# Hybrid decoder layer: low probability parts moved from VectorE to GpSimd, causal mask from a TensorE product to a VectorE addition in PSUM

## The chip, the core and the metric

The kernel is one program on one core of a Trainium2 chip. The core has TensorE (PE: matrix products, with its weight loads shown apart as PEld), VectorE (DVE), ScalarE (ACT), GpSimd (POOL) and SyncE (SP, which here only issues DMAs). Each engine works through its own queue in order; semaphores hold an instruction back until what it needs is there. The metric is the time on the device in microseconds (us), lower is better.

## What is computed

A decoder layer over 2048 tokens of width 1024, in fp32. The input is normalised and modulated, projected once, and feeds two attention branches: eight "forgetting" heads (causal softmax attention with a bias from cumulated log forget gates) and eight sliding-window heads. Each branch is gated, both go through one output projection, a second normalisation and a gated residual. The part that the change touches is the forgetting attention:

```python
def one_block(args):
    qb, cb, n = args                                   # 128 queries, their cumulated gate, block number
    s = jnp.einsum('bhqd,bhkd->bhqk', qb, kh, preferred_element_type=jnp.float32) * scale
    s = s + cb[..., None] - cum[:, :, None, :]
    q_pos = n * Q_BLOCK + jnp.arange(Q_BLOCK)
    causal = key_pos[None, :] <= q_pos[:, None]
    s = jnp.where(causal, s, -jnp.inf)
    p = jax.nn.softmax(s, axis=-1)
    return jnp.einsum('bhqk,bhkd->bhqd', p.astype(vh.dtype), vh)
```

## The kernel before

fp32 operands are split into two fp16 parts, a high part (the value rounded to fp16) and a low part (what the rounding left), and a product of two such operands is made of three fp16 products: high x high, high x low, low x high.

The program runs in stages: the modulation and the weights' splitting, the sliding-window branch, the forgetting branch (roughly 462 to 1000 us) and the rest of the output projection (to 1156 us). The forgetting branch also carries most of the projection work of the later heads, which is cut into small units and strewn between the attention's own instructions, so that PE always has something to do.

**Steps.** A forgetting head's 2048 queries are four chunks of 512 (`ci`). A step is one chunk against two blocks of 128 keys, with scores stored transposed: keys on the partitions, queries along the free dimension. Chunk `ci` has 2 x ci + 2 steps, a head 20, all eight heads 160. The last two steps of each chunk cross the diagonal: the first of them holds blocks with 512 and 384 valid queries (896 columns), the second 256 and 128 (384 columns); all others have 1024 columns. These 64 steps (2 x 4 x 8) are called masked steps here. `self.blocks` lists each block with its first valid sub-block `u0` and its column offset `o`.

**Life of a step** (class `Step`, line 1331 on):
- `scores` (L1339): for each of the two blocks two products into one PSUM tile `sta` (L1349 the low parts against the high ones, L1350 the rest with the gate's bias rows), and for a block on the diagonal a third, L1352: identity x `dmaskT`, a 128 x 128 constant with 0 where the key is allowed and -1e30 where it isn't, added into the block's first 128 columns. There is one `sta` tile (two banks), so the next step's scores wait until this step's exponential has read it.
- `exp32` (L1356, ACT): the exponential from PSUM to an fp32 tile `p`.
- `high` (L1360, ACT): `p` rounded to fp16, the first half of tile `pha`.
- `low` (L1363, DVE): `p` minus the rounded value, in fp16, the second half of `pha`. Both tiles have three buffers.
- `pv` (L1373, L1375, L1376, PE): the products with the values; L1376 reads the low part. After a chunk's last step come L1380 and L1382 (DVE: divide by the row sum) and `o_store` (L283): ACT rounds the output, DVE makes its low part (L291), SP stores it.

**Order of issue.** The program is written out by hand: the loop over `steps` at the end of the function puts each instruction on its engine's queue. One pass `s` issues: the exponential of step s; a `tick`, which issues what was put off by `after` (evacuations of finished units); the low part of step s-1; perhaps a part of the output weights' splitting (`w_out_split`, L1443 on DVE); the first half of this pass's units; the rounding of step s; the scores of step s+1; a second `tick`; the products of step s-2 with the values (`PV_LAG` is 2); the second half of the units. Units are projection units (`proj_units`, three products L351 each, evacuated by ACT and then DVE, L1073 or L392) and row-maximum units (`max_units`: a product L1300, reduced by DVE in L1303 or, for the block on the diagonal, L1305; after a chunk's last one `rows` combines them in L1312 to L1320). They share five PSUM banks.

**GpSimd's queue** holds in this stage only DMA issues: the gate's results (L394), the loads of later weights (L221), their row maxima out to DRAM (`w_max`, L230) and back as a broadcast (`w_back`, L235, which waits for the first to land), and the rows of the output gate (L1231, which wait for DVE to have used the last ones, L1237).

Of the kernel before, what the change touches and what calls it, by code (L numbers as in the profile page):

```python
# [16 lines left out]
ALU = mybir.AluOpType  # L17
AX = mybir.AxisListType

P = 128  # L20
# [15 lines left out]
XM, XR, VW = 66, 69, 129  # L36
# [7 lines left out]
def hybrid_layer(  # L44
# [17 lines left out]
    V, A, G, PE, SP = nc.vector, nc.scalar, nc.gpsimd, nc.tensor, nc.sync  # L62
# [94 lines left out]
    identb = const.tile([P, P], BF16, name="identb")  # L157
    identh = const.tile([P, P], F16, name="identh")
    dmaskT = const.tile([P, P], BF16, name="dmaskT")
# [26 lines left out]
    def bank(hold=False):  # L186
        n = next(n for n in order_ if n not in held)
        order_.remove(n)
        order_.append(n)
        if hold:  # L190
            held.add(n)
        return n
# [270 lines left out]
    start = ExitStack()  # L463
# [409 lines left out]
    class Pair:  # L873
# [7 lines left out]
        def scores(self):  # L881
            self.pss = ps_s.tile([P, 2, CH], F32, tag="s", name="pss")
            q = ab[self.j, self.i // 4]
            for e, (i, k0, nk) in enumerate(self.blocks):
                qo, o = (i % 4) * P, e * 2 * P + (2 - nk) * P
                for n, (a, b) in enumerate(((0, 0), (0, 1), (1, 0))):
                    for h in range(2):
                        r = slice(64 * h, 64 * h + 64)
                        PE.matmul(self.pss[:, h, o:o + nk * P], q[r, a, qo:qo + P],
                                  kst[self.g][r, b, k0 * P:(i + 1) * P], start=(n == 0), stop=(n == 2))  # L890
# [228 lines left out]
    def fill(n, each=None):  # L1119

        for _ in range(n):
            for f in events.pop(pos[0], []):
                f()
            punits[pos[0]]()
            pos[0] += 1
            if each:
                each()
# [120 lines left out]
    def const_rows(n, eng):  # L1248

        for slot, r0, r1 in ((0, 64, 66), (2, 66, 68), (0, 68, 69)):  # L1250
            eng.dma_start(Ts[n][r0:r1, slot, :].rearrange("p (u q) -> p u q", q=P),
                          fx["crow"][r0:r1, :].unsqueeze(1).broadcast_to([r1 - r0, NB, P]))
# [18 lines left out]
    def key_limbs(hd):  # L1271

        cv = sm(NB, "a_cv")
        V.tensor_scalar(cv[:], csum[:, hd, :], isc[f"qk{hd}"][:], None, op0=ALU.mult)
        for col, x_, nx in ((0, XA, True), (1, XB, True), (2, XC, False)):
            lc = lk[:, NB * col:NB * col + NB]
            V.tensor_scalar(lc, cv[:], 1.0 / x_, None, op0=ALU.mult)
            if nx:
                cv2 = sm(NB, "a_cv")
                V.scalar_tensor_tensor(cv2[:], lc, -x_, cv[:], op0=ALU.mult, op1=ALU.add)  # L1280
                cv = cv2
# [49 lines left out]
    class Step:  # L1331
# [9 lines left out]
        def scores(self):  # L1341
            T, ci = Ts[self.hd % 2], self.ci
            self.st = ps_st.tile([P, 2 * CH], F32, tag="st", name="sta")
            for b, u0, o in self.blocks:
                w = CH - u0 * P
                kb_ = slice(b * P, (b + 1) * P)
                qc = slice(ci * CH + u0 * P, (ci + 1) * CH)
                diag = b >= 4 * ci
                PE.matmul(self.st[:, o:o + w], T[:, 3, kb_], T[:, 1, qc], start=True, stop=False)  # L1349
                PE.matmul(self.st[:, o:o + w], T[0:XR, 2, kb_], T[0:XR, 0, qc], start=False, stop=not diag)  # L1350
                if diag:
                    PE.matmul(self.st[:, o:o + P], identb[:], dmaskT[:], start=False, stop=True)  # L1352

        def exp32(self):
            self.p32 = fxp.tile([P, 2 * CH], F32, tag="p32", name="p32")
# [4 lines left out]
            A.activation(self.ph[:, 0, :self.w], self.p32[:, :self.w], AF.Copy)  # L1360

        def low(self):
            V.tensor_tensor(self.ph[:, 1, :self.w], self.p32[:, :self.w], self.ph[:, 0, :self.w], op=ALU.subtract)  # L1363

        def pv(self):
            hd, ph = self.hd, self.ph
# [20 lines left out]
    steps = []  # L1387
# [247 lines left out]
    with tc.manual_schedule():  # L1635
        mi = 0
        V.memset(cmask[:], 0.0)
        V.tensor_copy(cmask[:, 3 * P:], dmask[:])
        const_rows(0, SP)
        const_rows(1, A)  # L1640
        key_limbs(0)
        fill(4, tick)
        pw_ = bk[bank()][:, 0:1]
        PE.matmul(pw_, ones[:], wsum[:], start=True, stop=True)
        root_scale(wrt[:], pw_)
        limbs1, ahead = False, 0
        while pos[0] < N_V3 or mi < M_LEAD:
            fill(1)
            if mi >= M_LEAD - 20 and mi % 2:
                fill(1)  # L1650
                ahead += 1
            if pos[0] == N_QK0 - 22:
                key_rows(0)
            if mi < M_LEAD and pos[0] >= N_QK0 - 12:
                munits[mi]()
                mi += 1
            if pos[0] >= N_V3 - 2 and not limbs1:
                key_limbs(1)
                limbs1 = True
            tick()  # L1660
        for _ in range(3):
            tick()
        key_rows(1)
        steps[0].scores()
        p0 = pos[0] - ahead
        p_tot = N_LAST - p0

        w_at, opened = {}, False
        w_all = sum(s.w for s in steps[:7 * NS])
        w_acc = 0  # L1670
        for s, stp_ in enumerate(steps):
            hd, r = divmod(s, NS)
            w_acc += stp_.w
            npn = p0 + min(p_tot, 14 + p_tot * w_acc // w_all) - pos[0]
            fil = fill
            if hd == 7 and r < 8:
                npn = N_LAST + (len(punits) - N_LAST) * (r + 1) // 8 - pos[0]
            if hd == 7 and r >= 8:
                npn, fil = N_IN * (r - 8) // (NS - 9) - opos[0], ofill
            m_goal = min(len(munits), M_LEAD + int(round((s + 1) * M_HEAD / NS)))  # L1680
            todo = []
            nmn = m_goal - mi
            a = b = 0
            while a < npn or b < nmn:
                if b >= nmn or (a < npn and a * nmn <= b * npn):
                    todo.append(lambda: fil(1))
                    a += 1
                else:
                    todo.append(munits[mi + b])
                    b += 1  # L1690
            mi = m_goal
            half = (len(todo) + 1) // 2
            if r == NS - 1 and hd + 2 < 8:
                key_limbs(hd + 2)
            stp_.exp32()
            tick()
            if s:
                steps[s - 1].low()
            for m in w_at.get(s, []):
                w_out_split(m)  # L1700
            for u in todo[:half]:
                u()
            stp_.high()
            if s + 1 < len(steps):
                steps[s + 1].scores()
            tick()
            for m in w_at.get(s + 3, []):
                w_out_load(m)
            if s >= PV_LAG:
                steps[s - PV_LAG].pv()  # L1710
            for u in todo[half:]:
                u()
            if r == NS - 1 and hd + 2 < 8:
                key_rows(hd + 2)
            if not opened and pos[0] >= N_OPEN and (r >= 14 or not late):
                while late:
                    tick()
                open_out()
                opened = True
                here = list(range(s + 3, 7 * NS))[:KT]  # L1720
                here += [7 * NS + n for n in (5, 6, 7, 8)][:KT - len(here)] + [7 * NS + n for n in range(9, 17)]
                w_at = {t: [m] for m, t in enumerate(here)}
                assert len(w_at) == 2 * KT
                w_out_load(0)
            if s == len(steps) - 2:
                outs[4].load()
                outs[5].load()
            if hd == 7 and r in (4, 6):
                outs[r // 2 - 2].load()
            if hd == 7 and r in (6, 8):  # L1730
                outs[r // 2 - 3].turn(3)
            if s % 8 == 0 and s // 8 < KT + 2:
                gate_load(s // 8)
            if s % 8 == 6 and s // 8 < KT + 2:
                gate_use(s // 8)
        assert pos[0] == len(punits) and mi == len(munits) and opos[0] == N_IN and not events
        tick()
        steps[-1].low()
        for n in range(PV_LAG, 0, -1):
            steps[-n].pv()  # L1740
        tick()
        tick()
        fxs.close()
        ozx = ExitStack()
        ozp = ozx.enter_context(tc.tile_pool(name="ozp", bufs=2, side="right", reuse_waits="tile"))
        ofill(len(ounits) - opos[0], tick2)
        for _ in range(4):
            tick()
# [35 lines left out]
```

## Time and profile before

| | |
|---|---|
| median of 3 runs | 1157.41 us (1156.38 to 1158.7) |
| profiled execution, its own time | 1157.8 us |
| span of that execution | 1156.1 us |
| busy over the whole span: PE / DVE / ACT / POOL | 97% / 80% / 57% / 18% |
| PE clock granted, mean | 0.996 |

The span runs from the first to the last instruction that the profiler recorded. A row of a group of instructions reads: line, engine, operation, output<-inputs with shapes, count | busy us in all, mean ns of one | idle us of the engine just before them, and what ended it. A row of waits reads: who waited <- for whom: us in total, times, longest. A row of a timeline reads: start in us, duration in us, engine, line, operation. Matmuls are pipelined: the duration of one overlaps the next one's.

### The profile page before, as it was taken

How to read it: one execution, taken by the hardware profiler on the slowest of the kernel's cores; microseconds unless marked ns; L12 is line 12 of the kernel's file. 1: busy time of each engine (PE TensorE's matmuls, PEld its weight loads, DVE VectorE, ACT ScalarE, POOL GpSimd, SP SyncE). 2: the span in 40 equal slices, each digit the busy share in tenths (PEclk: the TensorE clock that was granted, in tenths of full speed). 3: DMA queues.
4: the chain of work that ended last, by engine and by line, in shares of the span. 5: the costliest groups of instructions: out<-in, count | busy, mean ns of one | idle time of the engine just before them, and what ended most of it. 6: DMA issues, size and time to landing. Idle time of an engine off the chain costs nothing. (4 is left out here: it accounts for less than half of the span.)

```text
span 1156.1 us, 25291 instructions
## 1 busy us (share of the span) xinstructions
PE 1116.8 (97%) x9869; PEld 656.3 (57%) x9869; DVE 930.5 (80%) x2137; ACT 661.4 (57%) x1150; POOL 207.5 (18%) x332
## 2 busy tenths in 40 slices
PE   5899999999999999999999999999999999999997
PEld 2475544577765866555555555555555555544444
DVE  7877468987888568788988899888888887878885
ACT  2876344654555421666757666666776778534332
POOL 1122134554556530010010110001000000000000
PEclk9899999999999999999999999999999999999999
DMA  9943355433243232442344342123311337686743
GB/s 333 336 116 72 87 78 96 97 63 90 52 92 88 58 87 58 73 108 29 80 64 87 84 67 70 38 49 76 45 43 34 91 101 206 140 225 197 199 135 109
DMA packets 123476, 120.10 MB, mean 104 GB/s; under 512 B 64948, under 2 KB 100828, under 8 KB 123356
## 3 DMA queue, kind: packets, MB, share of 16 engines
q1 hardware_dynamic: 112088, 85.69, 27.6%
q0 software_dynamic: 10832, 32.50, 13.5%
q8 instruction: 77, 1.26, 0.6%
q14 instruction: 43, 0.35, 0.1%
q10 hardware_dynamic: 436, 0.28, 0.1%
HBM read 64.75 MB, written 25.18 MB: 78 GB/s over the span
## 5 line engine op out<-in xcount | busy, mean ns | idle before, releaser
L1356 ACT ACTIVATE p<-sta,lift,scl_qk 128x1024 f32<-128x1024 f32 (+2 forms) x160 | 172.0, 1075 | 131.6 <-PE sta L1350 82.6
L351 PE MATMUL bk<-hT,wh_qk 128*128 128x512 f16 x768 | 194.7, 378 | 0.0
L1363 DVE TENSOR_TENSOR pha<-p,pha 128x1024 f16<-128x1024 f32 (+2 forms) x160 | 169.1, 1057 | 0.2 <-ACT pha L1360 0.2
L1303 DVE TENSOR_REDUCE a_m<-bk 128x1 f32<-128x512 f32 x192 | 130.4, 686 | 45.8 <-PE bk L1300 44.8
L1576 PE MATMUL bk<-wohl,oz 128*128 128x512 f16 x744 | 165.3, 379 | 1.1 <-DVE oz L1525 0.7
L1360 ACT ACTIVATE pha<-p 128x1024 f16<-128x1024 f32 (+2 forms) x160 | 148.1, 926 | 5.9 <-PE poa L1376 1.2
L1576 PEld LDWEIGHTS <-oz 128*128 128x128 f16 x744 | 71.9, 99 | 82.8 <-DVE oz L1525 1.8
L1376 PE MATMUL poa<-vt,pha 128*128 128x65 f16 x1088 | 116.1, 192 | 1.4 <-DVE pha L1363 1.2
L1373 PE MATMUL poa<-vt,pha 128*128 128x65 f16 x1088 | 116.6, 193 | 0.8 <-DVE ona L1382 0.7
L1375 PE MATMUL poa<-vt,pha 128*128 128x64 f16 x1088 | 116.6, 194 | 0.0
L351 PEld LDWEIGHTS <-wh_qk 128*128 128x128 f16 x768 | 72.1, 97 | 74.4 <-issue 2.1
L1349 PE MATMUL sta<-T 128*128 128x512 f16 (+1 forms) x320 | 110.9, 346 | 2.8 <-ACT p L1356 2.7
L1300 PE MATMUL bk<-T 66*128 66x512 f16 (+2 forms) x320 | 109.7, 348 | 2.4 <-DVE a_m L1303 1.9
L1373 PEld LDWEIGHTS <-pha 128*128 128x128 f16 x1088 | 101.5, 96 | 15.5 <-DVE ona L1382 1.9
L1350 PE MATMUL sta<-T 69*128 69x512 f16 (+1 forms) x320 | 109.8, 348 | 0.0
L1375 PEld LDWEIGHTS <-pha 128*128 128x128 f16 x1088 | 100.9, 97 | 11.4
L1376 PEld LDWEIGHTS <-pha 128*128 128x128 f16 x1088 | 100.8, 99 | 1.8 <-DVE pha L1363 1.7
L351 PE MATMUL bk<-hT,wh_za 128*128 128x512 f16 x384 | 99.7, 378 | 0.0
L369 PE MATMUL bk<-wh_va,hT 128*128 128x256 f16 x768 | 91.9, 273 | 0.0
L351 PE MATMUL bk<-hT,wh_zb 128*128 128x512 f16 x384 | 91.6, 379 | 0.2 <-DVE qc L754 0.2
L351 PE MATMUL bk<-hT,wh_qb 128*128 128x512 f16 x384 | 91.2, 379 | 0.0
L369 PEld LDWEIGHTS <-hT 128*128 128x128 f16 x768 | 73.3, 98 | 12.2 <-issue 2.1
(459 smaller groups left out, 1919.7 us busy)
## 6 DMA issues: line engine op xcount, KB each, us to landing
hT<-in_x_dram SPq DMA_DIRECT2D x20, 512.0 KB
wa<-in_w_ada_dram SPq DMA_DIRECT2D x16, 512.0 KB
z_d<-tz POOLq DMA_DIRECT2D x32, 256.0 KB, 3.0
T<-z_d SPq DMA_DIRECT2D x16, 512.0 KB
T<-stq SPq DMA_DIRECT2D x62, 128.0 KB
out_dram<-hT SPq DMA_DIRECT2D x15, 512.0 KB
xt<-in_x_dram SPq DMA_DIRECT2D x12, 512.0 KB
qs<-qf SPq DMA_DIRECT2D x80, 64.0 KB
```

Source lines behind the costliest of these rows:

```text
L351: PE.matmul(ps, whl[:, a, k, :], hT[ci][:, b, k, :], start=(k == 0 and n == 0), stop=(k == KT - 1 and n == 2))
L369: PE.matmul(ps[:, (u % 2) * 2 * P:(u % 2 + 1) * 2 * P], hT[ci][:, a, k, u * P:(u + 1) * P], wv[p][:, b, k, :], start=(k == 0 and n == 0), ...
L1303: V.tensor_reduce(m3[:, u, pc:pc + 1], mx[:, :w], axis=AX.X, op=ALU.max)
L1349: PE.matmul(self.st[:, o:o + w], T[:, 3, kb_], T[:, 1, qc], start=True, stop=False)
L1350: PE.matmul(self.st[:, o:o + w], T[0:XR, 2, kb_], T[0:XR, 0, qc], start=False, stop=not diag)
L1356: A.activation(self.p32[:, :self.w], self.st[:, :self.w], AF.Exp, scale=scl[f"qk{self.hd}"][:], bias=lift[:])
L1360: A.activation(self.ph[:, 0, :self.w], self.p32[:, :self.w], AF.Copy)
L1363: V.tensor_tensor(self.ph[:, 1, :self.w], self.p32[:, :self.w], self.ph[:, 0, :self.w], op=ALU.subtract)
L1373: PE.matmul(po[:, u, :], ph[:, 0, pq], vt[:, b, hd, 0:65], start=(self.first and n == 0 and u == 0), stop=False)
L1375: PE.matmul(po[:, u, 0:64], ph[:, 0, pq], vt[:, b, hd, 65:VW], start=False, stop=False)
L1376: PE.matmul(po[:, u, :], ph[:, 1, pq], vt[:, b, hd, 0:65], start=False, stop=(self.last and n == len(self.blocks) - 1))
L1576: PE.matmul(py, self.hl[:, i, k, :], w_slot(8 * j + k)[:, cc], start=(k == 0 and m_ == 0), stop=(k == KT - 1 and m_ == 2))
```

## The change

The low part of the probabilities is made by GpSimd and issued directly behind the rounding of the same step, instead of by VectorE one pass later. The mask's two products per masked step go; in their place one VectorE instruction behind both blocks' products adds `dmaskT`, broadcast over two, to the first 128 columns of each block (the second block begins at column `o`), in place in PSUM. The exponential now waits for it in masked steps.

```diff
@@ scores
-                diag = b >= 4 * ci
                 PE.matmul(self.st[:, o:o + w], T[:, 3, kb_], T[:, 1, qc], start=True, stop=False)
-                PE.matmul(self.st[:, o:o + w], T[0:XR, 2, kb_], T[0:XR, 0, qc], start=False, stop=not diag)
-                if diag:
-                    PE.matmul(self.st[:, o:o + P], identb[:], dmaskT[:], start=False, stop=True)
+                PE.matmul(self.st[:, o:o + w], T[0:XR, 2, kb_], T[0:XR, 0, qc], start=False, stop=True)
+            b, u0, o = self.blocks[1]
+            if b >= 4 * ci:
+                d = self.st[:, 0:2 * o].rearrange("p (a c) -> p a c", a=2)[:, :, 0:P]
+                V.tensor_tensor(d, d, dmaskT[:].unsqueeze(1).broadcast_to([P, 2, P]), op=ALU.add)
@@ low
-            V.tensor_tensor(self.ph[:, 1, :self.w], self.p32[:, :self.w], self.ph[:, 0, :self.w], op=ALU.subtract)
+            G.tensor_tensor(self.ph[:, 1, :self.w], self.p32[:, :self.w], self.ph[:, 0, :self.w], op=ALU.subtract)
@@ the loop over steps
             stp_.exp32()
             tick()
-            if s:
-                steps[s - 1].low()
...
             stp_.high()
+            stp_.low()
             if s + 1 < len(steps):
                 steps[s + 1].scores()
...
         tick()
-        steps[-1].low()
         for n in range(PV_LAG, 0, -1):
             steps[-n].pv()
```

## The prediction

> **What bounds the kernel now.** I read the page's head first, then the busy times of the forgetting stage, then who waited for whom, and last the timelines of single steps.
>
> ```profile
> span 1156.1 us, 25291 instructions
> ```
> ```profile
> 462.00:994.00 532.00, 524.57 (x5408) 305.16 (x5407) 461.01 (x996) 377.60 (x460) 35.55 (x57) 1.00 0.34 74
> ```
>
> The second row is the stretch from 462 to 994 us, where all 160 forgetting steps run; its columns are length, then busy time of PE, PEld, DVE, ACT and POOL, the granted clock, the DMA share and GB/s. TensorE (PE) is busy for 524.6 of 532 us at the full clock, VectorE (DVE) for 87%, ScalarE (ACT) for 71%, GpSimd (POOL) for 7%. A step takes 532/160 = 3.3 us. A busy PE could still be a slow one, so I look at its waits.
>
> ```profile
> ACT p L1356 <- PE sta L1352: 44.3, 41, 4.6
> PE sta L1349 <- ACT p L1356: 2.7, 5, 0.7
> PE bk L1300 <- DVE a_m L1303: 1.7, 4, 0.7
> PE poa L1376 <- DVE pha L1363: 1.2, 2, 0.6
> ```
>
> These are rows of the waits (total us, times, longest). PE waited for DVE and ACT only 2.7 + 1.7 + 1.2 = 5.6 us in sum. The other direction is what matters: in 41 of the 64 masked steps the exponential on ACT was waiting for the last mask product. So the order of PE's stream sets the end, and whatever leaves that stream comes off the time, as long as no new wait takes its place.
>
> **What the removed products are worth.** One masked step on PE (start, duration):
>
> ```profile
> 747.53 0.22 PE L1352 MATMUL sta<-dmaskT,identb 128*128 128x128 bf16 x1
> 747.59 0.32 PE L1349 MATMUL sta<-T 128*128 128x384 f16 x1
> 747.75 0.33 PE L1350 MATMUL sta<-T 69*128 69x384 f16 x1
> 747.92 0.22 PE L1352 MATMUL sta<-dmaskT,identb 128*128 128x128 bf16 x1
> ...
> 749.82 0.27 PE L1349 MATMUL sta<-T 128*128 128x256 f16 x1
> ```
> ```profile
> L1352 PE MATMUL sta<-dmaskT,identb 128*128 128x128 bf16 x128 | 26.5, 219 | 0.0
> ```
>
> The group shows 26.5 us for 128 products, but each 0.22 us overlaps its neighbours: the next product starts 747.59 - 747.53 = 0.06 us later. What leaves the stream is 128 x 0.06 = 7.7 us, bounded by the resolution of the starts at 6.4 to 9.0 us (0.05 to 0.07 each). Its weight loads overlap other products and are not counted again.
>
> **What the low parts are worth.** They leave DVE:
>
> ```profile
> L1363 DVE TENSOR_TENSOR pha<-p,pha 128x1024 f16<-128x1024 f32 (+2 forms) x159 | 168.5, 1060 | 0.2 <-ACT pha L1360 0.2
> L1382 DVE TENSOR_TENSOR ona<-poa,a_ri 128x256 f32<-128x256 f32 x31 | 13.2, 424 | 1.1
> ```
>
> 168.5 us go, and 64 mask additions come. Each covers 2 x 128 columns of PSUM with a broadcast second operand, as L1382 does, so I price it at 0.42 us (26.9 us in all). DVE falls to 461.0 - 168.5 + 26.9 = 319 us of 532, or 60%. PE wins from that what it lost to DVE's lateness: 1.2 us of waits for low parts and part of the 1.7 us for freed banks. I take 2 us; the bounds are 0 and 5.6.
>
> On POOL the row nearest to the subtraction is a select with one input, 128x512:
>
> ```profile
> L934 POOL TENSOR_SCALAR_AFFINE_SELECT ptb<-fold x64: 624/640/1152, 165.3 to 409.7; 128x512 f16<-128x512 f16 x64
> ```
>
> Twice its median is 1.28 us for 1024 columns; if the second input costs as much again, 2.56 us. I take 2.1, nearer to the upper end because a subtraction does read two tensors. The steps hold 96 x 1024 + 32 x 896 + 32 x 384 = 139,264 columns, 136 full widths, so POOL gets 286 us, 54% of the stretch (174 to 348 us at the bounds). The probabilities are used two steps, some 6.7 us, after they are made, so a low part of 2.1 us right behind the rounding is in time, and the 7.7 us stay won on this side. The Trainium skill, GPSIMD Engine Reference, section 3 (Performance versus the Vector engine), measures 4497 ns for a two-input add over 2048 columns of fp32. That is an estimate of 2.25 us for 1024, and by it the sum below would end 1 us higher; no run here shows it yet.
>
> **What the mask addition costs.** The same step on the two engines behind PE (ACT, then DVE; the first ACT row is the rounding of the step before):
>
> ```profile
> 745.28 1.06 ACT L1360 ACTIVATE pha<-p 128x1024 f16<-128x1024 f32 x1
> ...
> 748.17 1.10 ACT L1356 ACTIVATE p<-sta,lift,scl_qk 128x896 f32<-128x896 f32 x1 [0.28 <-PE sta L1352]
> ...
> 750.48 0.67 ACT L1356 ACTIVATE p<-sta,lift,scl_qk 128x384 f32<-128x384 f32 x1 [0.22 <-PE sta L1352]
> ```
> ```profile
> 746.39 0.41 DVE L291 TENSOR_TENSOR oh<-ona,oh 128x256 f16<-128x256 f32 x1
> 746.72 1.22 DVE L1363 TENSOR_TENSOR pha<-p,pha 128x1024 f16<-128x1024 f32 x1
> 747.85 0.68 DVE L1303 TENSOR_REDUCE a_m<-bk 128x1 f32<-128x512 f32 x1
> ```
>
> There is one score tile, so the next scores (749.82) need this exponential to be over (748.17 + 1.10 = 749.27): the cover is 0.55 us. The addition takes 0.42 of it plus one more handover (0.04 us: the product's end at 747.92 + 0.22 = 748.14 to the exponential's start at 748.17). With DVE free at once, 0.09 us of cover is left and PE loses nothing. DVE is not free at once: it is busy 60% of the time, mostly with reductions of 0.7 us, so in 6 of 10 steps the addition waits some 0.35 us more and passes the cover by 0.26. The second masked step of a chunk has a shorter exponential (0.67 against 1.10) and so some 0.4 us more cover; only the first 32 pay: 32 x 0.6 x 0.26 = 5 us. Bounds: 0, and 64 x 0.26 = 17 us if every step paid. Behind the waiting addition on DVE's queue stand the reductions and evacuations of the next half step; PE has five banks for them, so they cost nothing.
>
> **What POOL does to DVE** is the part that I think decides. In the sliding-window stage POOL already worked beside DVE:
>
> ```profile
> L764 DVE TENSOR_TENSOR qs<-qs,sinT x20: 673/692/2251, 64.1 to 373.3; 128x512 f32<-128x512 f32 x20
> 267.38 2.19 DVE L764 TENSOR_TENSOR qs<-qs,sinT 128x512 f32<-128x512 f32 x1
> L897 DVE COPY_PREDICATED pss<-dmask,pss x32: 677/690/697, 153.8 to 394.5; 128x512 f32<-128x512 int16 x32
> ```
> ```profile
> 267.20 0.65 POOL L932 TENSOR_SCALAR_AFFINE_SELECT ptb<-fold 128x512 f16<-128x512 f16 x1
> ...
> 268.96 1.09 POOL L934 TENSOR_SCALAR_AFFINE_SELECT ptb<-fold 128x512 f16<-128x512 f16 x1
> ```
>
> The product of two SBUF tensors has a median of 692 ns; the one that began at 267.38, inside a run of four selects from 267.20 on, took 2.19 us and ended as the last select was finishing. L897, with one operand in PSUM, never took more than 697 ns. So a DVE instruction with two SBUF inputs stands still while POOL works, and one that reads PSUM doesn't: the mask addition itself is safe, but what stands ahead of it on the in-order queue isn't. These are the exposed ones of the stretch:
>
> ```profile
> L291 DVE TENSOR_TENSOR oh<-ona,oh 128x256 f16<-128x256 f32 x23 | 9.6, 418 | 0.0
> L1237 DVE SCALAR_TENSOR_TENSOR gacc<-gw,sil,gacc 128x1024 f32<-128x1024 f32 x7 | 8.9, 1277 | 0.0
> L273 DVE SCALAR_TENSOR_TENSOR wh_qk<-wr_qk,w_sw,wh_qk 128x512 f16<-128x512 f32 x12 | 8.9, 745 | 0.0
> L1443 DVE SCALAR_TENSOR_TENSOR wohl<-hT,wsc,wohl 128x512 f16<-128x512 f32 x8 | 6.0, 749 | 4.8 <-ACT wohl L1442 4.7
> L1443 DVE SCALAR_TENSOR_TENSOR wohl<-sv,wsc,wohl 128x512 f16<-128x512 f32 x8 | 6.0, 746 | 0.2 <-ACT wohl L1442 0.2
> L1319 DVE SCALAR_TENSOR_TENSOR a_mr<-lq,a_m 128x4 f32<-128x4 f16 x29 | 4.7, 163 | 1.0
> L273 DVE SCALAR_TENSOR_TENSOR wh_za<-wr_za,w_sw,wh_za 128x512 f16<-128x512 f32 x6 | 4.5, 745 | 0.0
> L1280 DVE SCALAR_TENSOR_TENSOR a_cv<-lk,a_cv 128x16 f32<-128x16 f16 x12 | 2.1, 175 | 0.4
> ```
>
> They are 23 + 7 + 12 + 8 + 8 + 29 + 6 + 12 = 105. POOL is busy 54% of the time, and the mean wait is half a mean low part (286/160/2 = 0.9 us): 105 x 0.54 x 0.9 = 51 us of DVE standing still. In steps without a mask DVE's free 40% absorbs it; 64 of 160 steps have one, which makes 20 us. Half I count as absorbed, by the wider cover of the short steps and because DVE catches up whenever PE waits: 10 us. Bounds: 0, and with lows of 2.56 us (POOL 65% busy, mean wait 1.09) 105 x 0.65 x 1.09 x 0.4 = 30 us.
>
> The example shows how it bites. The rounding ahead of it ends at 745.28 + 1.06 = 746.34, and POOL's low part would run from about 746.4 to 748.5, just where L291 begins (746.39). If POOL is first, L291 ends at 748.9, L1303 at 749.6, the addition at 750.0, the exponential at 751.1, and the next scores, due at 749.82, come 1.3 us late.
>
> The Trainium skill, SBUF — State Buffer, section Who interferes with whom, says that a VectorE instruction with two SBUF inputs contends with a GpSimd one that reads SBUF, as the rows above show, and that VectorE's 2-port copies and tensor_scalars do so too, with the loser blocked until the winner has finished. No row here shows the small tensor_scalars blocked. By the page the exposed count would rise by about the tensor_scalar steps of the same helper chains, some 75 instructions, and the 10 us to 17.
>
> POOL's other work is its DMA issues. The one that can hold the queue is the second half of a weight maximum, which waits on the first half's landing:
>
> ```profile
> PE bk L1576 11%; PE bk L1540 0%; PE bk L1514 0%; DVE T L1506 0%; DVE oz L1525 0%; DVE hT L1605 0%; DVE rs_t L113 0%; DVEq L1780 0%; DVE hT L1547 0%; ACT sv L1548 0%; DVE rs_y L119 0%; DVE y_rs L119 0%; DVE rs_v L103 0%; DVE rs_h L106 0%; DVE rs_y L107 0%
> POOL mxr L235 <- DMA mx_d<-w_mx: 45.1, 9, 9.0
> ```
>
> POOL sits there 9 times for 5 us (45.1/9) in the mean, but with nothing else to do; the two halves are ten projection units apart, some four steps, longer than the longest wait of 9.0 us, so with low parts in between little of it remains. I count nothing, and up to 9 x 1 us if it were not so. The first of these rows is the chain that ended last: it runs through the closing projection (L1576), which the change doesn't touch, so what the forgetting stage gains or loses arrives at the end unchanged.
>
> **Sum.** The profiled execution took 1157.8 us (span 1156.1 and 1.7 around it), 0.4 above the median of the runs shown. 1157.8 - 7.7 - 2 + 5 + 10 = 1163.1, and 1163 for a run.
>
> **The rivals.**
> 1. *The additions hide, the change pays* (other side). DVE with 40% free reaches the mask in time, and POOL's low parts seldom meet an exposed instruction: 1157.8 - 7.7 - 2 + 2 (additions) + 2 (contention) = 1152. For it speak DVE's relief of 142 us and that only 105 instructions are exposed; against it the cover of 0.55 us, of which the addition alone takes 0.46. The point from which it decides is a mean lateness of the mask of about 0.2 us.
> 2. *Gain and loss cancel*: the contention costs half of what I take, 1157.8 - 9.7 + 5 + 5 = 1158, no change that can be told.
> 3. *POOL becomes the bound.* From 532/136 = 3.9 us for a full width on, low parts fall behind and PE waits for each. At 4.6 us (four times the 1152 ns maximum of the select, as if POOL were always held up) it is 136 x 4.6 - 532 = 94 us, 1250. The medians speak against it.
> 4. *The products were not in PE's way*, so that nothing is gained and only 15 us paid: 1173. The starts 0.06 us apart speak against it.
>
> **How the numbers follow.** My forecast, slower by the late mask, gets 0.49, with its own range from 1160 to 1180; rival 1 gets 0.34, rival 2 0.12, rival 3 0.03, rival 4 0.02. A measurement tells 0.2%, 2.3 us, from no change. Faster is rival 1: 0.34; no change rival 2: 0.12; slower the rest: 0.54. The low end of the range takes in rival 1 with all of the 5.6 us won and little paid, 1157.8 - 7.7 - 4 + 2 = 1148; the high end the 30 us bound with half of the addition's 5: 1157.8 - 9.7 + 30 + 2.5 = 1181.
>
> **What would show it.** Right: the exponential of masked steps waits for DVE, PE's L1349 waits for the exponential far more than 2.7 us, and L291, L1237, L1443 have means well above 418, 1277 and 749 ns while L897-like instructions on PSUM keep theirs. Wrong: those means unchanged (no contention), a low part under 1.28 or over 2.56 us, PE's waits below 5 us, or a forgetting stage that is shorter by over 5 us.

## The result and the profile after

The changed kernel takes 1183.19 us in the median of 4 runs (1181.78 to 1185.45), the kernel before on the same chip 1157.17 (1156.38 to 1158.7): 2.27% more, ratio 1.0227 with a 95% interval of 1.0214 to 1.0239. The profiled execution took 1185.45 us; its span is 1183.7, 27.6 more than before. First the busy times from 462 us to the end of the forgetting stage and in two pieces of it (length, busy PE, PEld, DVE, ACT, POOL, granted clock, DMA share, GB/s):

```profile
462.00:1021.00 559.00, 525.56 (x5273) 300.06 (x5272) 387.16 (x899) 374.05 (x459) 330.97 (x215) 0.98 0.30 71
500.00:550.00 50.00, 45.05 (x433) 24.91 (x431) 35.24 (x70) 29.39 (x36) 29.41 (x21) 0.97 0.23 58
...
650.00:700.00 50.00, 46.34 (x447) 26.12 (x444) 36.97 (x73) 28.90 (x36) 31.15 (x23) 0.93 0.34 80
```

PE, which was busy for 524.6 of 532 us, is now busy for 525.6 of 559, and part of that at a lower clock. The waits of the changed kernel in the stage (total us, times, longest):

```profile
ACT p L1357 <- DVE sta L1353: 85.1, 43, 4.9
PE sta L1348 <- ACT p L1357: 29.2, 25, 5.2
```

In 43 masked steps the exponential waits for the mask, 2.0 us in the mean. In 25 steps PE's next scores then wait for the exponential, 29.2 us where there were 2.7; 20 of these steps are masked ones. No other wait of PE in the stage comes to 2 us. The groups on DVE that the prediction called exposed, with L1317, which it did not, then two that read PSUM, and the low parts on GpSimd (count | busy us, mean ns | idle before):

```profile
L291 DVE TENSOR_TENSOR oh<-ona,oh 128x256 f16<-128x256 f32 x23 | 23.2, 1008 | 0.2 <-ACT oh L295 0.2
L1317 DVE TENSOR_SCALAR lq<-a_m 128x4 f16<-128x4 f32 x29 | 17.0, 585 | 1.0
L1237 DVE SCALAR_TENSOR_TENSOR gacc<-gw,sil,gacc 128x1024 f32<-128x1024 f32 x7 | 12.7, 1817 | 0.0
L1444 DVE SCALAR_TENSOR_TENSOR wohl<-sv,wsc,wohl 128x512 f16<-128x512 f32 x8 | 8.4, 1051 | 4.4 <-ACT wohl L1443 4.4
L1319 DVE SCALAR_TENSOR_TENSOR a_mr<-lq,a_m 128x4 f32<-128x4 f16 x29 | 4.7, 163 | 1.0
...
L1303 DVE TENSOR_REDUCE a_m<-bk 128x1 f32<-128x512 f32 x175 | 119.1, 686 | 73.1 <-PE bk L1300 73.0
L1353 DVE TENSOR_TENSOR sta<-sta,dmaskT 128x256 f32<-128x256 f32 x63 | 27.4, 435 | 17.6 <-PE sta L1349 14.8 <-ACT pha L1361 2.3
```
```profile
L1364 POOL TENSOR_TENSOR pha<-p,pha x160: 900/2125/2747, 465.9 to 1025.0; 128x1024 f16<-128x1024 f32 x96, 128x896 f16<-128x896 f32 x32, 128x384 f16<-128x384 f32 x32
```

L291 went from 418 to 1008 ns, L1237 from 1277 to 1817, L1444 (L1443 before) from 746 to 1051. L1303, which reads PSUM, kept its 686 ns, and the mask takes 435. A low part takes 2125 ns in the median of all shapes, 2160 in the mean of the 96 full-width ones.

The worst step, the last but one of a chunk, shows how such a delay becomes a wait (start, duration):

```profile
943.82 2.13 POOL L1364 TENSOR_TENSOR pha<-p,pha 128x1024 f16<-128x1024 f32 x1 [0.44 <-ACT pha L1361]
...
944.83 1.14 DVE L1317 TENSOR_SCALAR lq<-a_m 128x4 f16<-128x4 f32 x1
...
945.42 0.33 PE L1349 MATMUL sta<-T 69*128 69x384 f16 x1
...
946.28 0.68 DVE L1303 TENSOR_REDUCE a_m<-bk 128x1 f32<-128x512 f32 x1
946.47 2.12 POOL L1364 TENSOR_TENSOR pha<-p,pha 128x1024 f16<-128x1024 f32 x1 [0.52 <-ACT pha L1361]
946.88 2.25 DVE L1444 SCALAR_TENSOR_TENSOR wohl<-sv,wsc,wohl 128x512 f16<-128x512 f32 x1
949.06 1.28 DVE L1303 TENSOR_REDUCE a_m<-bk 128x1 f32<-128x512 f32 x2
950.25 0.42 DVE L1353 TENSOR_TENSOR sta<-sta,dmaskT 128x256 f32<-128x256 f32 x1
950.77 1.10 ACT L1357 ACTIVATE p<-sta,lift,scl_qk 128x896 f32<-128x896 f32 x1 [4.44 <-DVE sta L1353]
951.92 0.37 PE L1348 MATMUL sta<-T 128*128 128x256 f16 x1 [5.24 <-ACT p L1357]
```

The scores are complete at 945.42 + 0.33 = 945.75. DVE is then in L1317, which ends with GpSimd's low part at 945.95 instead of after 0.17 us; L1444 starts 0.41 us after the next low part and ends half a microsecond behind it, 1.5 us late. Three reductions of 0.68 us stand in the queue as well. The mask comes 4.5 us after the scores, PE waits 5.24.

### The profile page after: what moved, and what is told of

It reads as the page before. It is cut to its first block, busy times and chain, and to the rows that moved or that the text cites. A ratio compares the mean times of both kernels' runs of the same rounds, so it can differ in the third digit from the quotient of the medians.

```text
span 1183.7 us, 25346 instructions
## 1 busy us (share of the span) xinstructions
PE 1120.3 (95%) x9741; PEld 652.9 (55%) x9741; DVE 856.8 (72%) x2041; ACT 659.8 (56%) x1150; POOL 505.5 (43%) x492
## 4 chain that ended last, share of the span: by engine, by line
PE 70%; DVE 12%; DMA 7%; ACT 5%; issue 4%; SPq 1%; POOL 0%; DVEq 0%; ACTq 0%; POOLq 0%
PE bk L351 25%; PE bk L1577 12%; PE bk L369 7%; PE sta L1348 5%; PE sta L1349 4%; PE bk L1300 4%; DMA wa<-in_w_ada_dram 2%; PE poa L1376 2%; PE poa L1377 2%; PE poa L1374 2%; ACT p L1357 2%; PE pss L889 1%; PE pob L946 1%; DVE a_m L1303 1%; DMA qs<-qf 1%
## 5 line engine op out<-in xcount | busy, mean ns | idle before, releaser
L1364 POOL TENSOR_TENSOR pha<-p,pha 128x1024 f16<-128x1024 f32 (+2 forms) x160 | 298.9, 1871 | 192.3 <-ACT pha L1361 175.3
L1303 DVE TENSOR_REDUCE a_m<-bk 128x1 f32<-128x512 f32 x192 | 130.6, 686 | 75.9 <-PE bk L1300 75.7
L1348 PE MATMUL sta<-T 128*128 128x512 f16 (+1 forms) x320 | 110.8, 351 | 29.9 <-ACT p L1357 29.6
L1305 DVE CUSTOM_DVE_ANT_0 bk<-bk,cmask 128x128 f32<-128x128 f32 (+3 forms) x128 | 63.2, 495 | 37.0 <-PE bk L1300 36.0
```

What stands on the lines that cost most here:

```text
L1364: G.tensor_tensor(self.ph[:, 1, :self.w], self.p32[:, :self.w], self.ph[:, 0, :self.w], op=ALU.subtract)
```

## The experiments

The theory under test, P, is the prediction's: GpSimd's reads hold VectorE up, and the mask waits behind what is held up. Its rival H: the mask is late by its place in VectorE's queue, whatever GpSimd does. Letters in later expectations stand for a theory and its rival in the same way. Ratios are to the kernel before, with 95% intervals.

**The two halves by themselves.** e1 moves only the low parts and keeps the mask's products. e2 only moves the mask and leaves the low parts on VectorE in their old place.

```diff
 e1: stop=not diag; if diag: PE.matmul(..., identb[:], dmaskT[:], ...)   # as before; no V.tensor_tensor
 e2:
-            G.tensor_tensor(self.ph[:, 1, :self.w], self.p32[:, :self.w], self.ph[:, 0, :self.w], op=ALU.subtract)
+            V.tensor_tensor(self.ph[:, 1, :self.w], self.p32[:, :self.w], self.ph[:, 0, :self.w], op=ALU.subtract)
...
+            if s:
+                steps[s - 1].low()
-            stp_.low()
```

> Only the low parts move to GpSimd; the mask stays a TensorE product. Theory P (port: GpSimd's reading of SBUF holds up VectorE instructions with two SBUF inputs, and these stand ahead of the mask addition): L291 is as slow as in the changed kernel (about 1000 ns against 418), but nothing on TensorE's path waits for VectorE, so the waits of the next scores for the exponential stay under 6 us and the time lies between 1152 and 1160 us. Rival H (handover: the addition on VectorE costs by itself, whatever GpSimd does): the same time, 1152 to 1160. Rival G (GpSimd's low parts are late for the products that use them): 1170 us or more.

> Only the mask moves to VectorE; the low parts stay there, in their old place. P: no port is contended (L291 at 418 ns), but VectorE is busy 92% of the forgetting stage and a low part of up to 1.2 us can stand ahead of the addition, so part of the lateness comes back by the queue alone: the next scores wait 8 to 20 us for the exponential, time 1158 to 1170. H: as in the changed kernel or worse, 1178 us or more.

e1: 1160.86 us, 1.0043 (1.0028 to 1.0058). e2: 1184.69 us, 1.0259 (1.0242 to 1.0276). The waits and L291 of e1, then of e2:

```profile
PE poa L1373 <- DVE ona L1382: 4.9, 2, 3.3
PE sta L1349 <- ACT p L1356: 3.2, 6, 0.8
```
```profile
L291 DVE TENSOR_TENSOR oh<-ona,oh 128x256 f16<-128x256 f32 x24 | 25.6, 1065 | 0.2 <-ACT oh L295 0.2
```
```profile
ACT p L1357 <- DVE sta L1353: 109.8, 51, 4.9
PE sta L1348 <- ACT p L1357: 31.6, 33, 4.8
```
```profile
L1364 DVE TENSOR_TENSOR pha<-p,pha 128x1024 f16<-128x1024 f32 (+2 forms) x158 | 167.3, 1059 | 0.2 <-ACT pha L1361 0.2
L291 DVE TENSOR_TENSOR oh<-ona,oh 128x256 f16<-128x256 f32 x23 | 9.6, 418 | 0.0
```

In e1 VectorE is held up as much as in the changed kernel (L291 at 1065 ns), but the scores' wait stays at 3.2 us (the time is 0.9 us above the expected range): contention alone costs 0.4%, with 4.9 us in two waits for a late division (L1382). e2 has no contention (L291 at 418), and the mask is later still, behind the low parts of 1.06 us that VectorE kept. This one went to H, against P's forecast. So the wait needs the mask on VectorE (e1) but not the contention (e2); what e2 and the changed kernel share is a mask behind something long.

**What GpSimd does to it.** e3 writes the low halves by two fills, so that GpSimd is about as busy (263 us against 299) but reads nothing; e8 copies, reading one tensor. Both leave out the low parts of the probabilities.

```diff
 e3:
-            G.tensor_tensor(self.ph[:, 1, :self.w], self.p32[:, :self.w], self.ph[:, 0, :self.w], op=ALU.subtract)
+            for _ in range(2):
+                G.memset(self.ph[:, 1, :self.w], 0.0)
 e8:
+            G.tensor_copy(self.ph[:, 1, :self.w], self.p32[:, :self.w])
```

> The changed kernel with each low part replaced by two memsets on GpSimd of the same size (the low parts of the probabilities are left out, zeros take their place): GpSimd stays busy, an estimated 1.5 to 2 us a step, but reads no SBUF. P: L291 and L1317 are back at about 418 and 170 ns, the next scores wait under 8 us for the exponential, time 1148 to 1157. H: waits and time as in the changed kernel, 1175 or more.

> The changed kernel with each low part replaced by one GpSimd copy of the exponentials into its tile (the low parts are left out, a copy takes their place): one SBUF input, an estimated 1.0 to 1.2 us for 1024 columns. Theory P (what holds VectorE up is that GpSimd reads SBUF): L291 and L1317 lie between their free and their held-up means (418 and 1008, 170 and 585 ns), the scores' wait between 10 us (memsets) and 29 us (subtraction), time 1162 to 1172. If only an instruction with two inputs holds the port: L291 at 418 ns and 1156 to 1159 us.

e3: 1157.41 us, 1.0015 (1.0006 to 1.0024). e8: 1162.82 us, 1.0045 (1.0030 to 1.0060). From e3, then from e8:

```profile
L1365 POOL MEMSET pha<- 128x1024 f16 (+2 forms) x320 | 263.1, 826 | 160.1 <-PE poa L1378 118.1 <-PE bk L1300 22.4 <-PE bk L1257 6.0
```
```profile
L291 DVE TENSOR_TENSOR oh<-ona,oh 128x256 f16<-128x256 f32 x24 | 10.0, 419 | 0.2 <-ACT oh L295 0.2
```
```profile
PE sta L1348 <- ACT p L1357: 10.3, 15, 2.8
```
```profile
L1364 POOL CAST pha<-p 128x1024 f16<-128x1024 f32 (+2 forms) x160 | 148.5, 930 | 274.2 <-ACT p L1357 243.3 <-PE bk L351 24.3 <-PE bk L1300 3.9
```
```profile
L291 DVE TENSOR_TENSOR oh<-ona,oh 128x256 f16<-128x256 f32 x24 | 17.3, 719 | 0.2 <-ACT oh L295 0.2
```
```profile
PE sta L1348 <- ACT p L1357: 14.1, 18, 3.5
```

With 263 us of fills L291 keeps its 419 ns; with 148 us of one-input reads it takes 719; with the subtractions 1008. The scores' wait follows: 10.3, 14.1, 29.2 us. e8 came out as P had it; e3 missed P's figures narrowly, 10.3 us against 8 and 1157.4 against 1157. Between e3 and the changed kernel lie 1.0227 - 1.0015 = 2.1%, some 24.5 us. They differ in what GpSimd reads, but also in how long it works and when: a fill waits for a free buffer (the first wait in its row), a subtraction for the rounding.

**Which instructions, and where the low parts stand.** e4 takes L291 and L1317 to L1320 from VectorE to GpSimd. h2 returns the 63 low parts whose next step is masked to VectorE, behind the mask. h4 is h2 with the mask's products back on PE in 17 steps (each head's first, and from step 138 on). h5 is h4 with all low parts on VectorE, one pass later and behind the next scores.

```diff
 e4:
+            (G if eng is SP else V).tensor_tensor(oh[:, :, 1], on, oh[:, :, 0], op=ALU.subtract)
+            G.tensor_scalar(lq_[:, 0:4], m4, -1.0 / XA, None, op0=ALU.mult)
...
 h2:
+            near = s + 1 < len(steps) and steps[s + 1].blocks[1][0] >= 4 * steps[s + 1].ci
+            if not near:
+                stp_.low()
             if s + 1 < len(steps):
                 steps[s + 1].scores()
+            if near:
+                stp_.low(V)
 h4: p_.on_pe = s % NS == 0 or s >= 138        # there the products, elsewhere the addition
 h5:
                 steps[s + 1].scores()
+            if s:
+                steps[s - 1].low()             # on VectorE
```

> The changed kernel with the two helper groups that were held up most taken off VectorE: the low part of the output (L291, 24 times) and the three small instructions that split the row maxima (L1317 to L1320, here four on GpSimd) run on GpSimd. P: the masks that came 1 to 4 us late come in time except behind the weights' and gate's splitting; the scores' wait falls from 30 us to 8 to 15, time 1160 to 1168. H: 1178 us or more.

> The changed kernel, but the low part of a step whose successor is masked (64 of 160) is made by VectorE again, issued behind the mask addition; the other 96 stay on GpSimd. P (port contention counts where a mask follows): the 20 us of waits between the memset kernel and the changed one mostly go, though 60% of GpSimd's work stays; scores' wait 10 to 16 us, time 1158 to 1165. Rival Z (VectorE's own load sets the lateness): 64 low parts back make it no better, 1175 or more.

> As the one above, and the mask stays a TensorE product in the first step of each head and from step 138 on, where VectorE's queue was longest even with memsets (splittings of key limbs, weight maxima, output weights). P: 5 us of products saved, waits near those of the kernel before: 1153 to 1160. Z: 1168 or more.

> GpSimd does no low parts: all are on VectorE, issued behind the next scores instead of ahead of them, and the mask is mixed as in the one above. P: no contention, VectorE 92% busy but with nothing large ahead of the mask: 1155 to 1166. Z: 1170 or more.

e4: 1174.8 us, 1.0168 (1.0150 to 1.0187). h2: 1172.25, 1.0130 (1.0115 to 1.0145). h4: 1162.55, 1.0045 (1.0030 to 1.0060). h5: 1169.92, 1.0109 (1.0092 to 1.0126). The scores' wait in e4, h2, h4 and, with a new one, h5:

```profile
PE sta L1349 <- ACT p L1358: 22.1, 19, 3.6
```
```profile
PE sta L1348 <- ACT p L1357: 20.1, 26, 3.7
```
```profile
PE sta L1348 <- ACT p L1360: 10.9, 19, 1.2
```
```profile
PE sta L1348 <- ACT p L1360: 10.0, 19, 1.1
PE poa L1380 <- DVE pha L1367: 5.4, 7, 1.7
```

All four came out above the first theory's figure, and below the rival's (h5 by 0.1 us only). e4 and h2 each take away a quarter to a third of the wait and leave the rest. h4 removes all waits of the scores over 1.2 us, but with part of the products back and GpSimd still reading it only comes near the kernel before. In h5 the low parts are late for their own products.

**More cover.** e5 gives the scores a second tile, for two of the five unit banks; e6 does that to the kernel before. k1 instead issues one unit more between a masked step's scores and the next ones where the next step has no mask, and one less where only the next step has one; k2 does that to the kernel before, k3 to e3.

```diff
 e5, e6:
-    ps_st = fox_pool("ps_st", 1, space=PSUM)
+    ps_st = fox_pool("ps_st", 2, space=PSUM)
-    bk += [ps_bx.tile([P, CH], F32, name=f"bk{n}") for n in (3, 4)]
 k1, k2, k3:
+            ma, mb = (p_.blocks[1][0] >= 4 * p_.ci for p_ in (stp_, steps[min(s + 1, len(steps) - 1)]))
+            half = min(len(todo), max(0, half + int(ma) - int(mb)))
```

> The changed kernel with two score tiles (four banks of PSUM instead of two) and three banks for the units instead of five. Theory Q (the mask comes late because of what stands ahead of it on VectorE's queue, own work and held-up work alike, and it costs TensorE only because one score tile leaves a cover of about half a microsecond): the wait of the next scores for the exponential falls from 29 us to under 5, whatever VectorE's lateness; with fewer unit banks some waits on them return, 5 to 15 us; time 1155 to 1170. Rival R (the lost time is not that cover: the late mask holds VectorE's later work, and TensorE would wait for that anyway): 1178 us or more.

> Control for the one above: the kernel before with two score tiles and three unit banks. Q and R alike: only the price of three banks for VectorE at 87%, 5 to 20 us, time 1162 to 1177; what e5 is above or below this is the change's own.

> The changed kernel, but with one unit more of TensorE's work behind the scores of a masked step that an unmasked one follows, and one less at the other end of the run, so that the exponential of a masked step has more cover. Cover theory: the late masks cost only what passes a cover of about half a microsecond, a unit adds 0.5 to 0.7 us for half of the masked steps, and of the 29.4 us that scores wait for the exponential some 10 to 15 go: 1166 to 1175. Rival (the lateness is work that VectorE has to catch up with, so that more cover only moves the wait): 1180 or more.

> Control: the kernel before with the same shift of one unit. Its scores wait only 2.7 us for the exponential, so the cover theory says 1154 to 1160, no change. If it is slower by over 5 us, the shift has a price of its own that has to come off the changed kernel's time too.

> The low parts of the probabilities left out (two GpSimd fills in their place), the mask on VectorE, and the shift of one unit. Without the shift this took 1157.4 with 10.3 us of scores waiting for the exponential. Cover theory: half of these go, 1150 to 1154, which would beat the kernel before. Rival: 1157 or more.

e5: 1195.09 us, 1.0337 (1.0320 to 1.0353). e6: 1195.13, 1.0327 (1.0310 to 1.0344). k1: 1177.3, 1.0190 (1.0174 to 1.0205). k2: 1158.01, 1.0020 (1.0011 to 1.0030). k3: 1156.77, 1.0011 (0.9999 to 1.0023). PE's largest waits in e5, all of those above 1.7 us in the stage, then the scores' wait in k1 and in k3:

```profile
PE bk L1297 <- DVE a_m L1300: 14.5, 14, 3.2
PE bk L1254 <- DVE a_m L1300: 5.7, 5, 2.6
PE bk L351 <- DVE a_m L1300: 3.3, 5, 1.1
```
```profile
PE sta L1348 <- ACT p L1357: 23.8, 24, 4.5
```
```profile
PE sta L1348 <- ACT p L1357: 10.1, 13, 2.2
```

With two score tiles no wait of the scores for the exponential is left, and the change costs nothing (e5 as e6); three unit banks cost both 3%, more than a second tile could return. Both missed their expectations (e5 came out where rival R had it, but so did its control), and it is no way out. It fits a loss that passes through the one score tile, but does not prove it: where PE waits for banks anyway, 23.5 us in these rows, other delays can hide. k1 lies between its two expectations: the wait fell by 5.4 us and the time by 0.4%, while the shift itself costs the kernel before 0.2%. The longest wait fell only from 5.2 to 4.5 us: one unit is small beside such a delay. k3 (low parts left out as in e3) still gains nothing that can be told: its scores wait 10.1 us, as long as in e3, where the cover theory had half of that gone.

**Other places for the work.** f1 is the kernel before with the mask's products replaced by a GpSimd select on the exponential (k4: with k1's shift). g1 is the changed kernel with the row-maximum units behind the projection units of a pass.

```diff
 f1:
+                d = self.p32[:, 0:2 * o].rearrange("p (a c) -> p a c", a=2)[:, :, 0:P]
+                G.affine_select(d, d, [[0, 2], [1, P]], ALU.is_ge, 0.0, base=0, channel_multiplier=-1)
 g1:
+            todo = [u for u in todo if u not in munits] + [u for u in todo if u in munits]
```

> The kernel before without the mask products; instead GpSimd zeroes the masked exponentials in SBUF (one select over 2 x 128 columns per masked step, between the exponential and the rounding); the low parts stay on VectorE. Q: nothing is added between the scores and the exponential, so the 7.4 us of products come off whole and the select (an estimated 0.5 to 0.7 us, from 640 ns for 512 columns) only delays the rounding, which has about two steps: 1148 to 1152 us. R makes no other forecast. If the rounding behind the select holds ScalarE's queue and with it the next exponential: 1153 to 1160.

> The mask as a GpSimd select on the exponential, the low parts on VectorE, and the shift of one unit. Without the shift 1157.5, with 7.3 us of scores waiting for the exponential. Cover theory: 1152 to 1156. Rival: 1157 or more.

> The changed kernel with each pass's row-maximum units put behind its projection units, so that most of their reductions and splittings stand behind the next mask on VectorE's queue instead of ahead. Q: of the 29 us of scores' waits those where L1303, L1305 and L1317 to L1320 stood ahead go, a third to a half: time 1166 to 1175. R: 1180 us or more.

f1: 1157.49 us, 1.0005 (0.9995 to 1.0014). k4: 1157.7, 1.0019 (1.0010 to 1.0029). g1: 1205.7, 1.0423 (1.0408 to 1.0439). f1's waits:

```profile
ACT pha L1361 <- POOL p L1357: 43.8, 51, 3.8
PE sta L1348 <- ACT p L1353: 7.3, 12, 1.0
```
In f1 the rounding on ScalarE waits for the select and the next exponentials come later. PE's scores wait 7.3 us against 2.7, which eats up most of what the products were worth. In k4 they wait as long (7.7 us), so there, too, the shift bought no cover. g1 was a wrong idea; why it lost another 2% was not followed up. No kernel tried was faster than the one before.

## Why the prediction was off

The direction and the mechanism were right, the size was not: 1163 forecast with 1148 to 1181, 1183 measured, and +5 where the profiled execution shows +27.6.

- **Products, 7.7 us.** Right in kind, somewhat too high. f1 leaves them out and runs its stage at the full clock, as the kernel before does:

```profile
461.00:993.00 532.00, 519.01 (x5278) 297.92 (x5277) 463.44 (x995) 374.81 (x459) 69.69 (x120) 1.00 0.33 74
```

  PE is busy for 519.0 us of a stretch in which it was busy for 524.6: 5.6 us, below the prediction's lower bound of 6.4. With 7.7, before's span gives 1156.1 - 7.7 + (10.3 - 2.7) = 1156.0 for e3, whose span is 1156.4, and 1159.8 against 1161.4 for e8; but both had 6.8 us at half clock in the stage, up to 3.4 us that these sums leave out. Rival 4 (products not in PE's way) is out, since PE's stream did get shorter.
- **Low parts on GpSimd, 2.1 us and 286 us in all.** Right: 2.16 us for a full width in the mean, 298.9 us for the 160, and no PE wait for one. Rival 3 is out.
- **PE's 2 us from a lighter VectorE.** Seen only without GpSimd's reads. PE's waits in the stage other than the scores' come to 4.4 us before, 2.1 in e3 and 4.0 in the changed kernel, and e1, which only moves the low parts, is 0.4% slower.
- **The addition itself, 0.42 us.** Right: 435 ns.
- **Its own-queue lateness, 5 us.** Too small, the lesser part of the miss. Without contention (e3) the scores' wait rose by 7.6 us. The step "only the first 32 pay" holds for 19.9 of the changed kernel's 29.6 us of stalls (0.4 of them after 1021 us), added up from PE's timeline by step; 5.8 stood behind second masked steps, as after 25 and 51, and 3.9 behind steps without a mask, where there were 2.1 before. A mean lateness of 0.35 us was the wrong model: five masked steps (138, 64, 24, 20, 25) carry 14.8 of the 29.6.
- **Contention, 10 us: the step that failed.** The 51 us of VectorE held up were sized about right: the four lines L291, L1317, L1237 and L1444 gained 23 x 0.590 + 29 x 0.415 + 7 x 0.540 + 8 x 0.305 + 8 x 0.288 = 34.1 us (L1317 stood at 170 ns before, and the second L1444 group went from 749 to 1037), and smaller groups bring it to some 49. That the total came out so close is in part luck: L1317 was not on the list, and the 29 of L1319, which were, gained nothing. What was wrong is the sentence "Half I count as absorbed". The scores' wait grew by 29.2 - 10.3 = 18.9 us from e3 to the changed kernel, which is the 20 us of "64 of 160 steps" with almost nothing absorbed; with the clock and the rest the two kernels are 24.5 us apart. The step at 945 us shows why: a delay ahead of a mask is spent once the 0.55 us of cover is gone, and then every further microsecond reaches PE. One more unit of cover (k1) returned 5.4 us of waits, not half of them.
- **The example.** The mechanism came as written, but in other steps: in step 84, from which it was worked out, L291 was in front this time.

```profile
762.86 0.41 DVE L291 TENSOR_TENSOR oh<-ona,oh 128x256 f16<-128x256 f32 x1
763.01 2.24 POOL L1364 TENSOR_TENSOR pha<-p,pha 128x1024 f16<-128x1024 f32 x1 [0.70 <-ACT pha L1361]
...
764.60 0.43 DVE L1353 TENSOR_TENSOR sta<-sta,dmaskT 128x256 f32<-128x256 f32 x1 [0.73 <-PE sta L1349]
```

- **The page's extra, "10 us to 17".** The Trainium skill, SBUF — State Buffer, section Who interferes with whom, had VectorE's tensor_scalars blocked too. The trace agrees in part: L1317, four columns wide with one SBUF input, went from 170 to 585 ns, but L1320 only to 231, and L1277 stayed at 175. Following that rule would have brought the forecast closer, to 1170, not to 1183.
- **Not in the sum: the clock.** 1157.8 - 7.7 + (29.2 - 2.7) = 1176.6, and 8.9 us are still missing to 1185.45. The next section accounts for up to 6.8 of them, and the products, 5.6 us instead of 7.7, for another 2.1. The forecast had no term for the clock.
- **Rival 1** asked for a mean lateness of the mask under 0.2 us. Without GpSimd's reads (e3, 1.0015), and with more cover on top (k3, 1.0011), the 7.7 us still do not show in the time. In both the scores' longer wait, some 10 us against 2.7, takes them. Rival 2 (gain and loss cancel) is out by the 2.27%.
- **The range.** Its high end counted 2.5 us for the addition where the working's own bound was 17; with that bound it would be 1157.8 - 9.7 + 30 + 17 = 1195 and hold the result. Its low end speaks of all 5.6 us won but takes off only 4; with 5.6 it is 1146.5.

## What to carry to other kernels

An instruction put between two engines on a chain with 0.5 us of cover pays for everything ahead of it in its in-order queue; price it by the longest things that can stand there, step by step, and count nothing as absorbed that no row shows. Work sent to GpSimd is paid for in the VectorE instructions that share its reads, so look at what waits behind those, not at VectorE's busy share: with the mask on PE the same contention cost 0.4%. Take away one cause at a time: low parts on VectorE or low parts on GpSimd, the mask was late with both.

## What the runs showed of the hardware

Three of the longest PE waits cost twice, since the clock was lower after them. Stretches of the changed kernel around the three places, and around a fourth wait, which had no such effect (549 to 552 us); the columns are those of the first view, with the granted clock third from the end:

```profile
531.99:535.40 3.41, 1.45 (x28) 1.18 (x28) 2.14 (x6) 2.41 (x4) 1.88 (x3) 1.00 0.24 57
535.40:538.81 3.41, 3.41 (x10) 1.21 (x9) 1.36 (x2) 0.88 (x2) 2.38 (x2) 0.50 0.02 4
...
549.05:552.46 3.41, 1.84 (x33) 1.44 (x33) 3.24 (x10) 2.05 (x2) 0.75 (x1) 1.00 0.77 160
688.99:692.40 3.41, 0.80 (x5) 0.28 (x4) 3.38 (x7) 0.57 (x1) 0.38 (x1) 1.00 0.17 28
692.40:699.20 6.80, 6.22 (x39) 3.44 (x39) 3.60 (x14) 2.67 (x4) 3.85 (x4) 0.50 0.62 123
944.99:948.40 3.41, 1.68 (x30) 1.23 (x29) 3.34 (x5) 1.33 (x2) 2.89 (x2) 1.00 0.44 143
948.40:951.80 3.40, 0.00 (x0) 0.00 (x0) 2.53 (x6) 1.03 (x2) 0.19 (x1) 0.50 0.00 0
951.80:955.20 3.40, 3.28 (x32) 2.33 (x32) 1.80 (x4) 3.17 (x7) 1.75 (x1) 0.50 0.00 1
```

The three stretches in which PE was busy for 1.45, 0.80 and 1.68 of 3.41 us were followed by half the clock for 3.4, 6.8 and 6.8 us; the one with 1.84 was not. That is 17.0 us at half clock, 3.4 of them with no PE work, so at most 13.6 / 2 = 6.8 us lost. The Trainium skill, TensorE: Matmul & The Clock Gate, Part 1, speaks of an idle window of about 3.4 us ahead of the lower clock; the windows ahead of the lower clock were not idle here, only less than half busy.

Beside GpSimd's subtractions of two tensors VectorE's two-input L291 took 1008 ns, beside its copies, which are half as long, 719, beside its fills 419, against 418 before. The one-input L1317 was slower beside fills as well, 241 ns against 170, and took 423 beside copies and 585 beside subtractions.
